# q and k of a dilated attention stored in three token orders, and score maxima over 65 rows instead of 64

## Chip, cores and metric

One core of one Trainium2 chip runs the whole program. The metric is the device time of one execution in microseconds (us), median over runs; lower is better.

## The reference

One encoder block on x of 1024 tokens and width 1024, all in float32. Cut to what the change touches, mixer A, an attention over strided neighbours:

```python
A_GROUPS = ((128, 1), (512, 4), (2048, 16))      # window, dilation; 4 heads of 64 per group

def dilated_group(q, k, v, window, dilation):
    L = S // dilation
    radius = window // (2 * dilation)            # 64 in all three groups
    def to_sub(t):
        return t.reshape(B, L, dilation, H, D).transpose(0, 2, 1, 3, 4).reshape(B * dilation, L, H, D)
    o, lse = banded_attention(to_sub(q), to_sub(k), to_sub(v), radius)
    ...

def mixer_dilated(qkv, pos):
    q, k = rotary(q, pos, ...), rotary(k, pos, ...)   # first 16 of 64 head dims
    ...                                               # 3 groups, combined by their softmax denominators
```

Around it: an input projection, a latent attention B with 8 heads, an output projection, and a feed-forward network with a squared relu.

## The kernel before

Products with large weights are split into a high and a low fp32r part, three matmuls for one, and run as a Strassen-like scheme of seven products (class `Seven`). The program has stages, one after the other: v and the rotary key (0 to about 97 us), the rest of the input projection, 17 units of 512 x 512 blocks (to 424.8 us), attention A with B's query projection woven in (to about 610 us), attention B, the output projection, and the feed-forward network.

**Projection units.** `proj.unit(u)` issues a unit's products in five steps and yields after each; the loop then issues a step of the next unit's operand preparation (`all_parts`: VectorE sums, a ScalarE cast to the high part, a GpSimd subtraction for the low part). Units 0 and 1 hold the rotary dims of q and k; in `put` a pair of their results takes 4 VectorE operations (L588 to L593) and 2 GpSimd products before it is stored. Units 2 to 5 hold the other q and k dims; `put` scales each of their four results with a VectorE product and stores it. Results lie as dims x tokens, in natural token order, in DRAM: `rx` (rotary) and `nx` (the rest).

**Attention A.** Four heads j, each with three groups g of dilation 1, 4 and 16 (g = 2 is computed as 8 residue classes with a parity mask). `load_qk(j, g)` brings Q and K (64 rows of dims, 1024 tokens) to SBUF; row 64 of K holds -1 and row 64 of Q the running maximum, so that the score product over 65 rows already subtracts it. For each head: `rounded` casts Q and K to fp32r; `maxima` multiplies the 64 rows and VectorE takes row maxima; `shift_a` turns them into Q's row 64, by 8 single-row operations for each group; `rows` copies that row to the Q of groups 1 and 2 by a DMA; `attend_a` computes scores (`scores`, two instructions for each fp32 product), exponentials, masks and the product with v. `shifts(j + 1)` is interleaved step by step with `attend_a(j)`, and between steps a fixed amount of TensorE work of B's query projection is issued (`ups.run`). The tokens of a block of g = 1 or 2 are 4 or 8 elements apart in Q and K:

```python
    def tokens(ap, g, b):
        ...
        d = 4 if g == 1 else 8
        v = ap.rearrange("p (i d) -> p d i", d=d)
        if g == 1:
            return v[:, b // 2, (b % 2) * P:(b % 2 + 1) * P]
        return v[:, b, :]
```

Each engine runs its instructions in the order of the program text; SyncE issues nearly all DMAs, in order.

Of the kernel before, what the change touches and what calls it, by code (L numbers as in the profile page):

```python
# [11 lines left out]
F32 = mybir.dt.float32  # L12
F32R = mybir.dt.float32r
# [4 lines left out]
P = 128  # L18
S = 1024
# [7 lines left out]
HA = 64  # L27
# [37 lines left out]
def tile_hybrid_block(ctx: ExitStack, tc: tile.TileContext, a: dict):  # L65
# [212 lines left out]


    vd = dram.tile([S, 6 * 192], F32, name="vd")  # L280
    rx = [dram.tile([192, S], F32, name=f"rx{i}") for i in range(2)]
    nx = dram.tile([1152, S], F32, name="nx")
    lat = [dram.tile([P, S], F32, name=f"lat{i}") for i in range(6)]


# [8 lines left out]
    X = {}  # L294
# [20 lines left out]
    halves = [slice(0, 512), slice(512, S)]  # L315
# [4 lines left out]
    def fetch_p(src):  # L320
        raw = raw_p(src.shape[-1])
        SP.dma_start(raw, src)
        return raw
# [180 lines left out]
    for k in range(HD):  # L504
# [1 line left out]
                      [lambda k=k: w_high("s3", W["a11"][k])],  # L506
                      [lambda k=k: w_low("s3", k, W["a11"][k])]])
    steps(items)
    proj = Seven(lambda u, e: fetch_p(a["w_p"][2 * u + e]), {n: (lambda k, n=n: (X[n][0][:, k], X[n][1][:, k]))
                  for n in ("b11", "b21", "b22", "t1", "t2", "t3", "t4")},  # L510
                 None, None, op_p, tmp_p, None)
    proj.fetch(0, 0, 1)
# [23 lines left out]

    NU = 17
    proj.first_parts(0)  # L540
    proj.first_parts(1)
    more = proj.all_parts(0, False)
# [30 lines left out]
    def scaled(u):  # L573

        return 2 <= u < 6 or u > 8

    def put(u, e, j, z, scale=True):

        tok = halves[j]
        if scale and scaled(u):  # L580
            V.tensor_mul(z, z, rbc[j])
        if u < 2:
            done[e, j] = z
            if (1 - e, j) in done:
                z1, z2 = done.pop((0, j)), done.pop((1, j))
                o = [tmp_p() for _ in range(4)]
                cos, sin = tabs[0][j], tabs[1][j]
                V.tensor_mul(o[0], z1, cos)  # L588
                G.tensor_mul(o[1], z2, sin)
                G.tensor_mul(o[2], z2, cos)  # L590
                V.tensor_mul(o[3], z1, sin)
                V.tensor_sub(o[0], o[0], o[1])
                V.tensor_add(o[2], o[2], o[3])  # L593
                for i, x in enumerate((o[0], o[2])):
                    SP.dma_start(rx[i][96 * u:96 * u + 96, tok], x[0:96])
                    n = 1024 + (2 * u + i) * 32
                    SP.dma_start(nx[n:n + 32, tok], x[96:128])
            return
        if u < 6:
            n = (2 * (u - 2) + e) * P  # L600
            SP.dma_start(nx[n:n + P, tok], z)
        elif u < 9:
            i = min(u - 6, 1)
            if u < 8 and e == j:
                C.activation(sums[i][j], z, AF.Square)
            else:
                s_ = work_p()
                C.activation(s_, z, AF.Square)
                G.tensor_add(sums[i][j], sums[i][j], s_)
            n = 2 * (u - 6) + e  # L610
            V.tensor_scalar(z, z, glat[:, n:n + 1], None, op0=ALU.mult)
            SP.dma_start(lat[n][:, tok], z)
        else:
            if last_unit:
                leave.append((zg[2 * (u - 9) + e][:, tok], z))
            else:
                SP.dma_start(zg[2 * (u - 9) + e][:, tok], z)

    def put_first(u, z):
        o = work_p()  # L620
        if scaled(u):
            V.tensor_mul(o, z, rbc[0])
        else:
            C.copy(o, z)
        put(u, 0, 0, o, False)

    proj.work, proj.first, proj.rest = work_p, put_first, put

# [13 lines left out]
    for u in range(NU):  # L642
        if u + 1 == NU:
            last_unit.append(u)
            for j in range(2):
                x = pop.tile([P, 512], F32, tag="op", name="rbc2", bufs=17)
                C.copy(x, rbc[j])
                rbc[j] = x
        if u + 2 < NU:
            proj.fetch(u + 2, 0, 1)  # L650
        more = proj.all_parts(u + 1, u + 1 >= 2) if u + 1 < NU else iter(())
        for _ in proj.unit(u, u >= 2, swap=u + 1 == NU):
            next(more, None)
            for _ in range(2):
                next(stats, None)
        if u == 0:
            put_first(1, proj.s1[1][0])
        if u == 9:
            stats = chain(mean_square(0, KVR, rkv), mean_square(1, QR, rq))
# [37 lines left out]
    def parts_g(raw, sub=G):  # L697
        return parts(raw, "wg", 1024, 4, sub)

    def tokens(ap, g, b):  # L700

        if g == 0:
            return ap[:, b * P:(b + 1) * P]
        d = 4 if g == 1 else 8
        v = ap.rearrange("p (i d) -> p d i", d=d)
        if g == 1:
            return v[:, b // 2, (b % 2) * P:(b % 2 + 1) * P]
        return v[:, b, :]


    QT, KTt, vt = {}, {}, {}

    def load_qk(j, g):
        for s_, (d, tag) in enumerate(((QT, "Q"), (KTt, "K"))):
            t_ = pqk.tile([HA + 1, S], F32, tag=tag, name=tag, bufs=5)
            d[j, g] = t_
            u = 6 * j + 3 * s_ + g
            for i in range(2):
                SP.dma_start(t_[8 * i:8 * i + 8], rx[i][8 * u:8 * u + 8])
            SP.dma_start(t_[16:HA], nx[48 * u:48 * u + 48])  # L720
        soon.append(lambda: G.memset(KTt[j, g][HA:HA + 1], -1.0))


    def load_v(g, pr):
# [10 lines left out]
        else:  # L735
            SP.dma_start(t_, src.rearrange("(p b) c -> p b c", b=TT))

    chores, soon = [], []
    q_raw, rots = {}, {}

    qd = [dram.tile([P, S], F32, name=f"qd{i}") for i in range(6)]
# [33 lines left out]
        return nq  # L775

    def rounded(j, g):
        qh = pr_.tile([HA, S], F32R, tag="qh", name="qh", bufs=2)
        kh = pr_.tile([HA, S], F32R, tag="kh", name="kh", bufs=2)
        (C.copy if (j, g) in ((0, 0), (0, 1), (2, 0)) else V.tensor_copy)(qh, QT[j, g][0:HA])  # L780
        C.copy(kh, KTt[j, g][0:HA])
        return qh, kh

    w_uq = [fetch(a["w_uq"][:, k * 768:k * 768 + 768]) for k in range(2)]
# [23 lines left out]
    for x in mgs:  # L808
        G.memset(x, 0.0)
    wuq += [parts(x) for x in w_uq[3:]]  # L810
    first = rounded(0, 0)
    while soon:
        soon.pop(0)()
    chores += [lambda: load_v(0, 0), lambda: load_qk(1, 0), lambda: load_qk(1, 1)]

    def band(b, n):
# [3 lines left out]
    def other(ap, g, b):  # L820

        n = TT if g == 0 else 2
        bb = b if g == 0 else b % 2
        lo, hi = band(bb, n)
        t0 = bb * P - 64 + lo
        if g == 0:
            return ap[:, t0:t0 + hi - lo]
        return ap.rearrange("p (i d) -> p d i", d=4)[:, b // 2, t0:t0 + hi - lo]


    def maxima(j, g, b0, qh, kh):

        n = 2 if g < 2 else 4
        pm = bank("ps_m").rearrange("p (b c) -> p b c", b=n)
        todo = []
        for b in range(b0, b0 + n):
            if g < 2:
                lo, hi = band(b if g == 0 else b % 2, TT if g == 0 else 2)
                mask, rhs = madd[:, lo:hi], other(kh, g, b)
            else:  # L840
                lo, hi, mask, rhs = 0, P, padd, tokens(kh, g, b)
            dst = pm[:, b % n, lo:hi]
            PE.matmul(dst, tokens(qh, g, b), rhs, start=True, stop=True)
            todo.append((b, dst, mask, hi - lo))
        for b, dst, mask, m in todo:
            junk = pa.tile([P, 256], F32, tag="junk", name="junk", bufs=1)
            V.tensor_tensor_reduce(out=junk[:, :m], in0=dst, in1=mask, scale=1.0, scalar=-BIG,
                                   op0=ALU.add, op1=ALU.max, accum_out=mgs[(3 * j + g) % 2][:, 32 * b:32 * b + 1])
# [16 lines left out]
                    V.tensor_max(mine, src, mine)  # L865

    def rows(j, g):
        SP.dma_start(QT[j, g][HA:HA + 1], QT[j, 0][HA:HA + 1])


    ROOM_MAX, ROOM_END, ROOM_SCORES = (800, 500, 460, 490), (2360, 2000, 2000, 1840), (260, 350, 350, 370)
# [19 lines left out]
    def attend_a(j):  # L891
# [21 lines left out]
        def scores(g, b0):  # L913
            pq = bank("ps_sA")
            pt = pa.tile([P, 512], F32, tag="pA", name="pA", bufs=4)
            q, k = QT[j, g], KTt[j, g]
            if g < 2:
                n = TT if g == 0 else 2
                for b in (b0, b0 + 1):
                    lo, hi = band(b if g == 0 else b % 2, n)  # L920
                    o = (b % 2) * 256
                    PE.matmul(pq[:, o + lo:o + hi], tokens(k, g, b), other(q, g, b), start=True, stop=True)
                f0 = band(b0 if g == 0 else 0, n)[0]
                f1 = 256 + band(b0 + 1 if g == 0 else 1, n)[1]
                C.activation(pt[:, f0:f1], pq[:, f0:f1], AF.Exp, scale=A_SCALE)
                keep_band(pt, f0, f1)
                return pt
            for b in range(b0, b0 + 4):
                o = (b % 4) * P
                PE.matmul(pq[:, o:o + P], tokens(k, g, b), tokens(q, g, b), start=True, stop=True)  # L930
            C.activation(pt, pq, AF.Exp, scale=A_SCALE)
            pt4 = pt.rearrange("p (b c) -> p b c", b=4)
            V.scalar_tensor_tensor(pt4, pt4, BIG, p01.unsqueeze(1).to_broadcast([P, 4, P]), op0=ALU.min, op1=ALU.mult)
            return pt
# [1216 lines left out]
```

## Time and profile before

| what | value |
|---|---|
| time, median of 3 runs (lowest to highest) | 1664.58 us (1663.78 to 1665.07) |
| the profiled execution: its time, its span | 1664.59 us, 1662.9 us |
| TensorE busy, share of the span | 1599.8 us, 96% |
| VectorE, ScalarE, GpSimd busy | 74%, 40%, 66% |
| moved by DMA | 208.16 MB, 125 GB/s |

The profile is of one execution. Engines are PE (TensorE matmuls), PEld (its weight loads, which overlap), DVE (VectorE), ACT (ScalarE), POOL (GpSimd) and SP (SyncE, which issues DMAs). L843 is line 843 of the kernel. Shares over the whole span hide the stages, so a change is read from the stage it lies in.

### The profile page before, as it was taken

The numbers are of one execution on the slowest core, as the hardware profiler recorded it, in microseconds if no ns is written. First come the engines' busy times: TensorE is split into PE (matmuls) and PEld (weight loads), VectorE is DVE, ScalarE is ACT, GpSimd is POOL, SyncE is SP. The second block draws the span as 40 slices with busy tenths as digits, with TensorE's granted clock in tenths as the row PEclk, the third lists the DMA queues.
The fourth block names the chain that finished last, engine by engine and source line by source line (L and its number), as shares of the span: only waits on it lengthen the run. The fifth ranks groups of instructions, "written<-read, shape, count | busy, mean of one in ns | idle before, by whom it ended". The sixth has DMA issues, their size and how long they took to land. (4 is left out here: it accounts for less than half of the span.)

```text
span 1662.9 us, 21207 instructions
## 1 busy us (share of the span) xinstructions
PE 1599.8 (96%) x7212; PEld 1327.3 (80%) x7212; DVE 1222.2 (74%) x1612; ACT 670.4 (40%) x1238; POOL 1103.7 (66%) x958
## 2 busy tenths in 40 slices
PE   7889999999999999999899999799999999999997
PEld 7778888888788887777678887688888888888886
DVE  8967556454646678889977267997776789889885
ACT  5732233222333347666666344322222363343421
POOL 7757457544724358777767346787777778888865
PEclk9899999999989899999999999899999999999999
DMA  6533233232644200000026243354434385445352
GB/s 231 165 124 129 108 108 116 94 126 101 192 128 121 67 17 20 20 1 20 20 99 224 101 165 114 122 178 176 146 140 158 139 310 164 140 141 160 119 201 101
DMA packets 85643, 208.16 MB, mean 125 GB/s; under 512 B 10472, under 2 KB 23968, under 8 KB 85536
## 3 DMA queue, kind: packets, MB, share of 16 engines
q1 hardware_dynamic: 85536, 206.82, 36.8%
q8 instruction: 57, 0.93, 0.2%
q14 instruction: 50, 0.41, 0.1%
HBM read 143.54 MB, written 63.18 MB: 124 GB/s over the span
## 5 line engine op out<-in xcount | busy, mean ns | idle before, releaser
L1276 POOL TENSOR_TENSOR pl<-pf,ph 128x512 fp32r<-128x512 f32 x124 | 168.4, 1364 | 56.7 <-DVE ph L1275 35.5
L103 POOL TENSOR_TENSOR op_p<-tS_p,op_p 128x512 fp32r<-128x512 f32 x68 | 94.9, 1416 | 103.6 <-ACT op_p L102 103.6
L1896 PE MATMUL ps_y<-opl,oph 128*128 128x512 f32 x364 | 141.8, 390 | 0.0
L1896 PE MATMUL ps_y<-oph 128*128 128x512 f32 x364 | 141.7, 389 | 0.0
L1896 PE MATMUL ps_y<-oph,opl 128*128 128x512 f32 x364 | 141.6, 389 | 0.0
L1981 DVE TENSOR_TENSOR R<-R,ps_y 128x1024 f32<-128x1024 f32 x84 | 100.8, 1213 | 22.6 <-PE ps_y L1896 22.4
L1854 DVE TENSOR_TENSOR opl<-raw_u,oph 128x512 fp32r<-128x512 f32 x91 | 110.5, 1242 | 7.3 <-ACT oph L1849 7.0
L103 POOL TENSOR_TENSOR opl<-tS,oph 128x512 fp32r<-128x512 f32 x61 | 94.1, 1562 | 28.3 <-ACT oph L102 24.5
L1271 ACT ACTIVATE pf<-ps_sB 128x512 f32<-128x512 f32 x128 | 76.6, 598 | 69.6 <-PE ps_sB L110 60.6
L102 ACT CAST op_p<-tS_p 128x512 fp32r<-128x512 f32 x68 | 39.9, 618 | 144.0 <-DVE tS_p L195 81.6
L1148 DVE TENSOR_REDUCE mx<-ps_mB 128x1 f32<-128x512 f32 x128 | 81.0, 682 | 17.0 <-PE ps_mB L1146 16.7
L103 POOL TENSOR_TENSOR op_p<-raw_p,op_p 128x512 fp32r<-128x512 f32 x51 | 72.8, 1433 | 21.2 <-ACT op_p L102 17.6
L1854 POOL TENSOR_TENSOR opl<-wk,oph 128x512 fp32r<-128x512 f32 x52 | 82.2, 1606 | 3.1 <-ACT oph L1849 2.9
L103 POOL TENSOR_TENSOR opl<-raw_f,oph 128x512 fp32r<-128x512 f32 x48 | 80.5, 1690 | 4.2 <-ACT oph L102 3.7
L1854 POOL TENSOR_TENSOR opl<-raw_f,oph 128x512 fp32r<-128x512 f32 x39 | 57.3, 1486 | 38.2 <-PE ps_y L1896 30.6
L1849 ACT CAST oph<-wk 128x512 fp32r<-128x512 f32 x52 | 32.3, 621 | 122.3 <-POOL wk L1821 49.3
L1896 PEld LDWEIGHTS ps_y<-opl,oph 128*128 128x128 f32 x364 | 68.3, 188 | 14.8 <-POOL opl L1854 0.6
L1896 PEld LDWEIGHTS ps_y<-oph 128*128 128x128 f32 x364 | 68.3, 188 | 14.6 <-ACT R L1985 0.5
L1896 PEld LDWEIGHTS ps_y<-oph,opl 128*128 128x128 f32 x364 | 68.3, 188 | 14.1
L152 PE MATMUL ps_zb<-Tl,oph 128*128 128x512 f32 x192 | 75.8, 395 | 2.7 <-DVE Tl L103 2.7
L151 PE MATMUL ps_zb<-Th,oph 128*128 128x512 f32 x192 | 75.7, 394 | 2.9 <-DVE wk L216 1.8
L153 PE MATMUL ps_zb<-Th,opl 128*128 128x512 f32 x192 | 75.7, 394 | 0.0
(492 smaller groups left out, 5174.5 us busy)
## 6 DMA issues: line engine op xcount, KB each, us to landing
raw_f<-in_w_ff SPq DMA_DIRECT2D x68, 512.0 KB
raw_u<-ua SPq DMA_DIRECT2D x39, 512.0 KB
raw_p<-in_w_p SPq DMA_DIRECT2D x34, 512.0 KB
ua<-su SPq DMA_DIRECT2D x26, 512.0 KB
ua<-uo SPq DMA_DIRECT2D x43, 256.0 KB
sg<-zg SPq DMA_DIRECT2D x32, 256.0 KB
zg<-wk SPq DMA_DIRECT2D x28, 256.0 KB
wk<-in_xT SPq DMA_DIRECT2D x16, 256.0 KB
```

Source lines behind the costliest of these rows:

```text
L102: C.copy(hi, src)
L103: (sub or V).tensor_sub(lo, src, f32(hi))
L151: PE.matmul(out, wh[:, c], bh, start=first and k == 0, stop=False, skip_group_check=True)
L152: PE.matmul(out, wh[:, c], bl, start=False, stop=False, skip_group_check=True)
L153: PE.matmul(out, wl[:, c], bh, start=False, stop=k == 3, skip_group_check=True)
L1148: V.reduce_max(mx[h][:, hf, t:t + 1], pq, axis=AX.X)
L1271: C.activation(pf, pq, AF.Exp, scale=B_SCALE)
L1276: sub.tensor_sub(pl, pf, f32(ph))
L1849: C.copy(hi, x)
L1854: eng.tensor_sub(lo, x, f32(hi))
L1896: PE.matmul(out, l[:, col], r_, start=first and p == 0 and e == 0, stop=p == len(CHUNKS[c]) - 1 and e == 2, skip_group_check=True)
L1981: V.tensor_add(acc, acc, py2)
```

## The change

1. `put_qk` stores every q and k result in three token orders. The natural order is stored at once. Two ScalarE copies, each to a fresh 128 x 512 buffer, put the tokens into the order of dilation 4 and 8 and store those; they are queued and issued when two steps of the unit loop have been counted (`turned_qk`), ahead of the next operand preparation. 48 copies and 64 stores are new.
2. The units run in the order 2, 3, 0, 4, 1, 5, then 6 to 16: the rotary units are third and fifth.
3. `load_qk` reads Q and K of a group in that group's order, for g = 2 by two DMAs in pieces of 64 tokens where one DMA read whole rows. `tokens` and `other` become contiguous slices.
4. `rows` is a ScalarE copy of one row into the group's order instead of a DMA.
5. `rounded` casts 65 rows, and so `maxima` multiplies 65. Q's row 64 is set to 0 by a GpSimd memset behind that of K's; the first `rounded` moves behind these memsets.

```diff
-    rx = [dram.tile([192, S], F32, name=f"rx{i}") for i in range(2)]
-    nx = dram.tile([1152, S], F32, name="nx")
+    rx = [[dram.tile([192, S], F32, name=f"rx{g}{i}") for i in range(2)] for g in range(3)]
+    nx = [dram.tile([1152, S], F32, name=f"nx{g}") for g in range(3)]
...
+    UNITS = [2, 3, 0, 4, 1, 5] + list(range(6, NU))
...
+    def put_qk(j, x, *to):
+        for dst, n, a, b in to:
+            SP.dma_start(dst[0][n:n + b - a, halves[j]], x[a:b])
+        def turn(g):
+            d = 4 * g
+            t_ = work_p()
+            C.copy(t_.rearrange("p (d i) -> p d i", d=d), x.rearrange("p (i d) -> p d i", d=d))
+            ...
+        turns.append([2, lambda: turn(1)])
+        turns.append([2, lambda: turn(2)])
...
         for _ in proj.unit(u, u >= 2, swap=u + 1 == NU):
+            turned_qk()
             next(more, None)
...
     def load_qk(j, g):
...
-                SP.dma_start(t_[8 * i:8 * i + 8], rx[i][8 * u:8 * u + 8])
-            SP.dma_start(t_[16:HA], nx[48 * u:48 * u + 48])
-        soon.append(lambda: G.memset(KTt[j, g][HA:HA + 1], -1.0))
+                fetch_rows(t_[8 * i:8 * i + 8], rx[g][i][8 * u:8 * u + 8], g)
+            fetch_rows(t_[16:HA], nx[g][48 * u:48 * u + 48], g)
+        def last_rows():
+            G.memset(KTt[j, g][HA:HA + 1], -1.0)
+            G.memset(QT[j, g][HA:HA + 1], 0.0)
+            has_rows.add((j, g))
+        soon.append(last_rows)
...
     def rounded(j, g):
-        qh = pr_.tile([HA, S], F32R, tag="qh", name="qh", bufs=2)
+        qh = pr_.tile([HA + 1, S], F32R, tag="qh", name="qh", bufs=2)
...
-    first = rounded(0, 0)
     while soon:
         soon.pop(0)()
+    first = rounded(0, 0)
...
-            PE.matmul(dst, tokens(qh, g, b), rhs, start=True, stop=True)
+            PE.matmul(dst, tokens(qh, b), rhs, start=True, stop=True)
...
     def rows(j, g):
-        SP.dma_start(QT[j, g][HA:HA + 1], QT[j, 0][HA:HA + 1])
+        d = 4 * g
+        src, dst = QT[j, 0][HA:HA + 1], QT[j, g][HA:HA + 1]
+        C.copy(dst.rearrange("p (d i) -> p d i", d=d), src.rearrange("p (i d) -> p d i", d=d))
```

**What moves on the engines.** First GpSimd at the start of attention A, around the memsets of K's row 64 (L721). Before:

```order
L103 TENSOR_TENSOR Wl<-raw,Wh 128x768
L721 MEMSET K 1x1024 x3
L103 TENSOR_TENSOR qp<-stage,qp 128x512 x2
L990 TENSOR_TENSOR ropes<-kpe,ropes 128x128
L991 TENSOR_TENSOR ropes<-kpe,ropes 128x4x16
```

With the change:

```order
L103 TENSOR_TENSOR Wl<-raw,Wh 128x768
L757 MEMSET K 1x1024
L758 MEMSET Q 1x1024
L757 MEMSET K 1x1024
L758 MEMSET Q 1x1024
L757 MEMSET K 1x1024
L758 MEMSET Q 1x1024
L103 TENSOR_TENSOR qp<-stage,qp 128x512 x2
```

Six memsets stand where three stood, and the cast that feeds the first maxima (qh, ScalarE) now waits for the first two of them, where it waited for no GpSimd instruction.

Second VectorE in the first unit, from the preparation of the next unit's sums (L195, L196) to the second unit's first result (the second L216). Before:

```order
L195 TENSOR_TENSOR tS_p<-raw_p 128x512
L196 TENSOR_TENSOR tS_p<-raw_p,tS_p 128x512
L232 TENSOR_TENSOR wk<-wk,ps_zc 128x512
L588 TENSOR_TENSOR tS_p<-wk 128x512
L591 TENSOR_TENSOR tS_p<-wk 128x512
L592 TENSOR_TENSOR tS_p<-tS_p 128x512
L593 TENSOR_TENSOR tS_p<-tS_p 128x512
L237 TENSOR_TENSOR wk<-wk,ps_zb 128x512
L588 TENSOR_TENSOR tS_p<-wk 128x512
L591 TENSOR_TENSOR tS_p<-wk 128x512
L592 TENSOR_TENSOR tS_p<-tS_p 128x512
L593 TENSOR_TENSOR tS_p<-tS_p 128x512
```

With the change:

```order
L195 TENSOR_TENSOR tS_p<-raw_p 128x512
L196 TENSOR_TENSOR tS_p<-raw_p,tS_p 128x512
L232 TENSOR_TENSOR wk<-wk,ps_zc 128x512
L614 TENSOR_TENSOR wk<-wk,oA 128x512
L237 TENSOR_TENSOR wk<-wk,ps_zb 128x512
L614 TENSOR_TENSOR wk<-wk,oA 128x512
L652 TENSOR_TENSOR wk<-ps_z_1007,oA 128x512
L216 TENSOR_TENSOR wk<-wk,ps_zb 128x512
```

Between L232 and the next L216 stand four operations, where nine stood.

## Rows read from the trace of the kernel before

**Rows 1.** The page, part 1: busy time of each engine, share, instructions.

```profile
PE 1599.8 (96%) x7212; PEld 1327.3 (80%) x7212; DVE 1222.2 (74%) x1612; ACT 670.4 (40%) x1238; POOL 1103.7 (66%) x958
```

**Rows 2.** Stretches: length; busy PE, PEld, DVE, ACT, POOL; clock, DMA share, GB/s.

```profile
117.00:124.00 7.00, 0.59 (x3) 0.18 (x2) 7.00 (x8) 0.00 (x0) 6.20 (x4) 0.69 0.28 83
124.00:130.00 6.00, 5.99 (x14) 4.73 (x15) 2.73 (x4) 1.66 (x3) 3.92 (x4) 0.51 0.72 218
130.00:160.00 30.00, 30.00 (x134) 24.83 (x133) 26.00 (x26) 7.38 (x13) 23.95 (x16) 1.00 0.37 121
...
425.00:451.00 26.00, 22.79 (x142) 19.61 (x141) 20.50 (x73) 8.96 (x18) 19.65 (x25) 1.00 0.76 206
...
454.00:468.00 14.00, 14.00 (x51) 11.42 (x50) 3.73 (x14) 2.67 (x4) 4.59 (x18) 0.51 0.77 237
...
498.50:539.80 41.30, 39.69 (x221) 34.31 (x222) 24.80 (x80) 13.62 (x25) 18.46 (x41) 1.00 0.43 122
...
570.00:581.00 11.00, 11.00 (x47) 10.55 (x47) 7.79 (x29) 1.71 (x4) 2.51 (x2) 0.53 0.00 1
```

**Rows 3.** TensorE's timeline, a step of group 0: start, length, engine, what.

```profile
500.33 1.03 PE L922 MATMUL ps_sA<-Q,K 65*128 65x256 f32 x4
501.29 0.50 PE L843 MATMUL ps_m<-kh,qh 64*128 64x256 f32 x2
501.72 0.38 PE L108 MATMUL ps_uq<-qp,Wh 128*128 128x256 f32 x1
501.94 0.28 PE L109 MATMUL ps_uq<-qp,Wh 128*128 128x256 f32 x1
502.06 0.28 PE L110 MATMUL ps_uq<-qp,Wl 128*128 128x256 f32 x1
```

**Rows 4.** TensorE's timeline, a step of group 1.

```profile
508.43 1.63 PE L922 MATMUL ps_sA<-Q,K 65*128 65x192 f32 x4
509.99 0.77 PE L843 MATMUL ps_m<-kh,qh 64*128 64x192 f32 x2
510.69 0.39 PE L108 MATMUL ps_uq<-qp,Wh 128*128 128x256 f32 x1
```

**Rows 5.** TensorE's timeline, a step of group 2.

```profile
523.71 2.12 PE L930 MATMUL ps_sA<-Q,K 65*128 65x128 f32 x8
525.76 1.21 PE L843 MATMUL ps_m<-kh,qh 64*128 64x128 f32 x4
526.90 0.39 PE L108 MATMUL ps_uq<-qp,Wh 128*128 128x256 f32 x1
```

**Rows 6.** TensorE's timeline, scores of the last head, before a 96-row product.

```profile
583.39 2.72 PE L922 MATMUL ps_sA<-Q,K 65*128 65x192 f32 x12
585.76 0.81 PE L1146 MATMUL ps_mB<-KTh,QTh 96*128 96x512 f32 x2
```

**Rows 7.** Timelines of ScalarE, VectorE and TensorE around TensorE's idle time in the projection.

```profile
102.94 1.07 ACT L569 COPY oA<-ps_r 128x512 f32<-128x512 f32 x2
...
113.58 1.78 DVE L592 TENSOR_TENSOR tS_p<-tS_p 128x512 f32<-128x512 f32 x1
...
117.20 0.39 PE L153 MATMUL ps_zc<-x_t1h,op_p 128*128 128x512 f32 x1
124.01 0.77 PE L151 MATMUL ps_zb<-x_t3h,op_p 128*128 128x512 f32 x1 [6.42 <-DVE wk L216]
```

**Rows 8.** ScalarE in the projection, 130 to 280 us, by line: busy us, mean ns.

```profile
L162 ACT COPY wk<-ps_z 128x512 f32<-128x512 f32 x8 | 4.7, 584 | 19.7 <-PE ps_z L153 19.7
```

**Rows 9.** The start of attention A, timelines of GpSimd, ScalarE and TensorE.

```profile
425.70 2.73 POOL L721 MEMSET K<- 1x1024 f32 x3
...
423.11 1.05 ACT L781 CAST kh<-K 64x1024 fp32r<-64x1024 f32 x1
...
424.76 0.49 PE L843 MATMUL ps_m<-kh,qh 64*128 64x192 f32 x2
```

**Rows 10.** A load for group 2 and the cast that needs it, timelines of SyncE and ScalarE.

```profile
507.18 0.62 SPq L719 DMA_DIRECT2D Q<-rx  x2
...
518.36 1.04 ACT L781 CAST kh<-K 64x1024 fp32r<-64x1024 f32 x1
```

More of the change, by code (lines that the diff above doesn't have):

```diff
@@ L508, in tile_hybrid_block @@
     steps(items)
-    proj = Seven(lambda u, e: fetch_p(a["w_p"][2 * u + e]), {n: (lambda k, n=n: (X[n][0][:, k], X[n][1][:, k]))
+    NU = 17
+    UNITS = [2, 3, 0, 4, 1, 5] + list(range(6, NU))
+    proj = Seven(lambda i, e: fetch_p(a["w_p"][2 * UNITS[i] + e]), {n: (lambda k, n=n: (X[n][0][:, k], X[n][1][:, k]))
                   for n in ("b11", "b21", "b22", "t1", "t2", "t3", "t4")},
@@ L535, in tile_hybrid_block @@
             SP.dma_start(x, a["rot_a"][i][:, h])
-    NU = 17
     proj.first_parts(0)
@@ L575, in scaled, with turned_qk, put @@
         return 2 <= u < 6 or u > 8
-    def put(u, e, j, z, scale=True):
+    turns = []
+    def put_qk(j, x, *to):
[5 more added lines that the diff above has]
+            C.copy(t_.rearrange("p (d i) -> p d i", d=d), x.rearrange("p (i d) -> p d i", d=d))
+            for dst, n, a, b in to:
+                rows = dst[g][n:n + b - a]
+                if g == 1:
+                    SP.dma_start(rows.rearrange("p (d j i) -> p d j i", d=d, j=2)[:, :, j],
+                                 t_[a:b].rearrange("p (d i) -> p d i", d=d))
+                else:
+                    SP.dma_start(rows[:, halves[j]], t_[a:b])
+        turns.append([2, lambda: turn(1)])
+        turns.append([2, lambda: turn(2)])
+    def turned_qk():
+        for t_ in turns:
+            t_[0] -= 1
+        while turns and turns[0][0] <= 0:
+            turns.pop(0)[1]()
+    def put(i, e, j, z, scale=True):
+        u = UNITS[i]
         tok = halves[j]
@@ L594, in put @@
                 for i, x in enumerate((o[0], o[2])):
-                    SP.dma_start(rx[i][96 * u:96 * u + 96, tok], x[0:96])
-                    n = 1024 + (2 * u + i) * 32
-                    SP.dma_start(nx[n:n + 32, tok], x[96:128])
+                    put_qk(j, x, ([r_[i] for r_ in rx], 96 * u, 0, 96), (nx, 1024 + (2 * u + i) * 32, 96, 128))
             return
         if u < 6:
-            n = (2 * (u - 2) + e) * P
-            SP.dma_start(nx[n:n + P, tok], z)
+            put_qk(j, z, (nx, (2 * (u - 2) + e) * P, 0, P))
         elif u < 9:
@@ L617, in put, with put_first @@
                 SP.dma_start(zg[2 * (u - 9) + e][:, tok], z)
-    def put_first(u, z):
+    def put_first(i, z):
         o = work_p()
-        if scaled(u):
+        if scaled(UNITS[i]):
             V.tensor_mul(o, z, rbc[0])
@@ L624, in put_first @@
             C.copy(o, z)
-        put(u, 0, 0, o, False)
+        put(i, 0, 0, o, False)
     proj.work, proj.first, proj.rest = work_p, put_first, put
@@ L698, in parts_g, with tokens, fetch_rows @@
         return parts(raw, "wg", 1024, 4, sub)
[L700 to L708, printed above, removed]
-    QT, KTt, vt = {}, {}, {}
+    def tokens(ap, b):
+        return ap[:, b * P:(b + 1) * P]
+    QT, KTt, vt = {}, {}, {}
+    def fetch_rows(dst, src, g):
+        if g == 2:
+            src = src.rearrange("p (j d i) -> p d j i", j=2, d=8)
+            dst = dst.rearrange("p (d j i) -> p d j i", j=2, d=8)
+            for h in range(2):
+                SP.dma_start(dst[:, :, h], src[:, :, h])
+            return
+        SP.dma_start(dst, src)
     def load_qk(j, g):
@@ L736, in load_v @@
             SP.dma_start(t_, src.rearrange("(p b) c -> p b c", b=TT))
-    chores, soon = [], []
+    chores, soon, has_rows = [], [], set()
     q_raw, rots = {}, {}
@@ L777, in rounded @@
     def rounded(j, g):
-        qh = pr_.tile([HA, S], F32R, tag="qh", name="qh", bufs=2)
-        kh = pr_.tile([HA, S], F32R, tag="kh", name="kh", bufs=2)
-        (C.copy if (j, g) in ((0, 0), (0, 1), (2, 0)) else V.tensor_copy)(qh, QT[j, g][0:HA])
-        C.copy(kh, KTt[j, g][0:HA])
+        assert (j, g) in has_rows
+        qh = pr_.tile([HA + 1, S], F32R, tag="qh", name="qh", bufs=2)
+        kh = pr_.tile([HA + 1, S], F32R, tag="kh", name="kh", bufs=2)
+        (C.copy if (j, g) in ((0, 0), (0, 1), (2, 0)) else V.tensor_copy)(qh, QT[j, g])
+        C.copy(kh, KTt[j, g])
         return qh, kh
@@ L827, in other @@
             return ap[:, t0:t0 + hi - lo]
-        return ap.rearrange("p (i d) -> p d i", d=4)[:, b // 2, t0:t0 + hi - lo]
+        return ap.rearrange("p (d i) -> p d i", d=4)[:, b // 2, t0:t0 + hi - lo]
     def maxima(j, g, b0, qh, kh):
@@ L840, in maxima @@
             else:
-                lo, hi, mask, rhs = 0, P, padd, tokens(kh, g, b)
+                lo, hi, mask, rhs = 0, P, padd, tokens(kh, b)
             dst = pm[:, b % n, lo:hi]
-            PE.matmul(dst, tokens(qh, g, b), rhs, start=True, stop=True)
+            PE.matmul(dst, tokens(qh, b), rhs, start=True, stop=True)
             todo.append((b, dst, mask, hi - lo))
@@ L921, in scores @@
                     o = (b % 2) * 256
-                    PE.matmul(pq[:, o + lo:o + hi], tokens(k, g, b), other(q, g, b), start=True, stop=True)
+                    PE.matmul(pq[:, o + lo:o + hi], tokens(k, b), other(q, g, b), start=True, stop=True)
                 f0 = band(b0 if g == 0 else 0, n)[0]
@@ L929, in scores @@
                 o = (b % 4) * P
-                PE.matmul(pq[:, o:o + P], tokens(k, g, b), tokens(q, g, b), start=True, stop=True)
+                PE.matmul(pq[:, o:o + P], tokens(k, b), tokens(q, b), start=True, stop=True)
             C.activation(pt, pq, AF.Exp, scale=A_SCALE)
```

## Prediction

> **What bounds the kernel now.** I read the page's engine line first: TensorE is busy 96% of the span, the next engine 74% [rows 1]. So a gain has to come out of TensorE's own time, or out of the few places where it waits. The table of stretches then shows the stages that the change touches: the projection, with one stretch where TensorE stands (117 to 124 us, 0.59 of 7 us busy), and attention A from 425 us on, with TensorE busy 39.69 of 41.30 us in the second head while VectorE has 24.80, ScalarE 13.62 and GpSimd 18.46 [rows 2]. A is bound by TensorE too, but by what? TensorE's timeline answers that. Starts of neighbouring rows tell what an instruction really costs, since the lengths overlap.
>
> Three things are to be seen there. **First**, a product over 64 rows does not overlap with its neighbours. Two products of 256 columns follow each other in 0.12 us (L109 to L110), but the pair of maxima takes 0.43 us (501.29 to 501.72), the first product behind it 0.22 instead of 0.12, and the four scores before it 0.96 us [rows 3]. Twelve contiguous scores in the last head (2 of 192 columns, 10 of 256, 2944 together) take 2.37 us, 0.805 ns for a column, and the 96-row product behind them starts without such a delay [rows 6]; by that price four of 256 columns take 0.82 us. So a group-0 call of maxima loses 0.19 + 0.10 + 0.14, about 0.4 us, to the change from and to 64 rows. The scores have 65 rows and lose nothing against 128-row neighbours. **Second**, strided reads cost more. Four group-1 scores of 192 columns take 1.56 us (508.43 to 509.99) where contiguous ones would take 4 x 0.155 = 0.62; a pair of maxima takes 0.70 [rows 4]. Eight group-2 scores take 2.05 us, 0.256 each; four maxima take 1.14 [rows 5]. **Third**, in the first projection unit VectorE works through a run of rotary operations at up to 1.78 us each, and the product that waits for it starts 6.42 us late [rows 7]; the 6 us behind it run at a granted clock of 0.51 [rows 2], the 1.2 GHz level.
>
> **The change, part by part.** The sum is made against the profiled execution, 1664.59 us, which is the median (1664.58) to 0.01 us.
>
> *Maxima and scores on TensorE.* Contiguous products of few columns cost no less than 0.12 us, the nearest row [rows 3]. There are 16 group-0 calls, 16 group-1 calls and 8 group-2 calls of maxima, and 16 and 8 groups of scores of groups 1 and 2.
> - Group-0 maxima: 16 x 0.4 = 6.4.
> - Group-1 maxima: 0.70 - 0.24 = 0.46, and 0.10 behind them: 16 x 0.56 = 9.0.
> - Group-2 maxima: 1.14 - 0.48 = 0.66, and 0.10: 8 x 0.76 = 6.1.
> - Group-1 scores: 1.56 - 0.62 = 0.94: 16 x 0.94 = 15.0.
> - Group-2 scores: 2.05 - 8 x 0.12 = 1.09: 8 x 1.09 = 8.7.
>
> That is 45.2 us at full clock. In the last head no maxima follow the scores (0.6 less), and stretches such as 454 to 468 and 570 to 581 us run at half clock [rows 2], where part of a slow read is hidden under slower columns. The ends are 39, if the groups in these 25 of A's 182 us gain nothing, and 45; I take 42, between them, since only a part is hidden. An extra 65th row costs nothing, as the 65-row scores show.
>
> *Units in another order.* The rotary operations leave the first unit, with five products of some 2.7 us; VectorE has four operations between L232 and L216 there instead of nine. The 6.42 us go, and 0.49 of the 6 us at half clock, 2.9 us: 9.3. What is late next: the first result is now scaled by VectorE with a factor that a ScalarE copy delivers only at about 103.5 us (102.94 plus half of 1.07) [rows 7], and L216 stands behind it. Nothing shows that wait before; it is between 0 and two contended VectorE operations, 3.6 us. I take 2. In the third and fifth unit the rotary run meets units of seven products, 19 us instead of 13.6. The second rotary unit of before, next to such a unit, left TensorE busy 30.00 of 30 us [rows 2], so I count 0 to 3 and take 1. Together -6.
>
> *48 ScalarE copies of 128 x 512, 8 in each of six units.* A contiguous copy takes 0.584 us [rows 8]. None with a step of 16 or 32 bytes is in the trace; below that price nothing is likely, and above it the nearest row is TensorE's own ratio for a step of 32 bytes, 0.256 to 0.12: 1.25 us. I take 0.8, nearer to the same engine's row: 6.4 us for each unit. The cover is ScalarE's idle time: it is busy 7.38 of 30 us [rows 2], 4.7 of a 19-us unit, and operands are prepared one unit ahead. So 0 on the path, at 1.25 us too (10 of 14.3 free). If the cover is gone, each copy is paid in full. The rows above show that strided reads are slow for TensorE. The Trainium skill, SBUF — State Buffer, section Door 1: The DMA port swizzle, gives 16-byte lines as the reason: reads that touch each line once pay a penalty, which would hold for these copies as well. It names no price for ScalarE, and with TensorE's ratio the sum would stay as it is; with a higher price it is the last rival below.
>
> *64 new stores and smaller loads.* The stores queue on SyncE, at about 0.31 us for an issue [rows 10]; no engine waits for them, except ScalarE for a buffer that comes round again. The load for a later head's group 2 has twelve DMAs instead of six. Two issues take 0.62 us, so the last one goes out some 2 us later; it starts at 507.18 and the cast that needs it ran at 518.36 [rows 10], 11 us later. Shorter steps leave about 8. Covered: 0; if not, 1 to 2 us for each of three heads.
>
> *Row copies and memsets.* Eight single-row ScalarE copies of 1024 elements, near the 1.05 us of a 64-row cast [rows 9], to 2.2 by the same ratio, lie under ScalarE's idle time in A (13.62 of 41.30 busy); so do 12 more memsets of 0.91 us on GpSimd (18.46 of 41.30) [rows 2]. 0.
>
> *The first maxima wait for memsets.* This is a new wait on the path. At 424.76 TensorE starts its first maxima, 0.6 us after the casts. The memsets start at 425.70 behind the last weight subtraction, at 0.91 us each [rows 9]. The casts now wait for two, until 427.5, and take 1.05 each, so TensorE starts at about 429.7: **5 us** late, and everything behind it in the queue with it. After 6.4 us of idle time the clock was at half for 6 us and 2.9 us were lost [rows 2]; I add 3. The ends are 4 and 12 (14 us at half clock, as at 454). Together +8.
>
> *Clock in A.* Stretches at 0.51 and 0.53 cost about half of 14 and 11 us, 12 us in all [rows 2]. The later one lies in strided group-2 steps, before which TensorE had not stood idle; with short steps it may go. Ends 0 and -12; I take -3.
>
> *New waits in A.* A head with 41.30 us loses 4 x (0.4 + 0.56 + 0.94) + 2 x (0.76 + 1.09) = 11.3, leaving 30 for 24.80 us of VectorE [rows 2], 83%. Some steps will wait for VectorE; ends 0 and 20, I take +5.
>
> Sum: -42 - 6 + 8 - 3 + 5 = **-38**, so 1664.6 - 38 = **1627 us**.
>
> **The rivals.**
> - *VectorE becomes the bound.* If it cannot go over 70% of a stretch, each of three heads stays at 24.8 / 0.7 = 35 us instead of 30, and 425 to 451 us, with VectorE already at 20.50 of 26, saves nothing of its 5.4: 20 us of waits instead of 5, **1642 us**. For it: those 20.50 us. Against: TensorE rarely waits for VectorE in A now, and at the end of a head only.
> - *The drain stays at 65 rows.* The maxima follow f32r products and the scores f32 ones, so the loss could hang on something else than 64 rows. Then 40 calls x 0.4 = 16 us stay: **1643 us**. The 65-row scores and the 96-row product [rows 6] speak against it. This is the case that the change does not do what it says.
> - *Everything is recovered.* The clock stays at full behind the first maxima and in A, and nothing new waits: -45 - 9 + 5 - 5 = -54, **1611 us**.
> - *The other side: ScalarE becomes the bound of the projection.* Its copies have room for 1.8 us each in four units and 1.28 in the first two (13.6 less 3.4 of other work, by 8). Beyond that TensorE pays 48 S - 78 for S us a copy; this eats the 38 us from S = 2.4, four times a contiguous copy. At 3 us it is +66, **1693 us**. For it speaks that strided reads are slow and that no row prices them on ScalarE; against, that TensorE's own ratio is 2.1, half of what it takes.
>
> **How the numbers follow.** The chances are 0.50 for the forecast (its own range 1619 to 1635), 0.20 for VectorE, 0.08 for the drain, 0.15 for full recovery, 0.05 for ScalarE, and 0.02 for a mixture that ends near no change. The range of 0.8 reaches from 1612, just short of full recovery, to 1646, over the two cases near 1642. About 0.2% (3.3 us) is what a measurement of this kernel can tell from no change. All cases but the last two lie below 1661: faster 0.93, same 0.02, slower 0.05.
>
> **What would show it.** In the profile of the changed kernel: group-1 and group-2 scores four and eight in about 0.65 and 0.95 us; maxima in 0.12 us each, with no delay behind them; no idle 6.4 us near 117; a ScalarE copy under 1.3 us; TensorE idle for about 5 us before its first maxima; VectorE at 80% or more of each head. The prediction is wrong if maxima over 65 rows still take 0.2 us each, if the copies take over 2 us, or if A shortens by less than 20 us.

## Result, and the profile after

The changed kernel takes **1640.38 us** (median of 4 runs, 1633.53 to 1643.42) against 1664.78 us for the kernel before, run beside it: ratio 0.985, 95% interval 0.9817 to 0.988. The forecast was 1627 us, so 24 of the 38 us arrived. The profiled execution took 1641.31 us with a span of 1639.4 us, 23.4 us less than before.

The page, part 1, of the changed kernel, answers to [rows 1]:

```profile
PE 1566.1 (96%) x7212; PEld 1306.0 (80%) x7212; DVE 1231.2 (75%) x1612; ACT 738.6 (45%) x1294; POOL 1120.5 (68%) x970
```

TensorE's busy time fell by 33.7 us and the span by 23.4: some 10 us more of it are idle. To see where, I cut both traces at the first maxima and at the first scores of B. The table of stretches (columns as in [rows 2]) for attention A before:

```profile
424.76:613.74 188.98, 181.93 (x948) 158.38 (x947) 116.41 (x348) 62.52 (x129) 84.08 (x205) 0.92 0.37 106
```

And after, with the projection's stretches, then A, then four stretches within A:

```profile
117.00:124.00 7.00, 7.00 (x33) 5.79 (x32) 5.56 (x6) 7.00 (x9) 4.80 (x4) 1.00 0.98 292
124.00:130.00 6.00, 6.00 (x28) 4.99 (x27) 4.49 (x5) 4.54 (x8) 5.97 (x5) 1.00 0.91 317
...
421.02:590.43 169.41, 154.25 (x946) 146.03 (x947) 116.48 (x346) 79.37 (x137) 92.34 (x212) 0.83 0.41 115
446.40:460.10 13.70, 13.70 (x55) 12.78 (x53) 4.92 (x19) 6.93 (x7) 5.77 (x18) 0.50 0.79 245
483.90:497.60 13.70, 13.70 (x55) 12.94 (x55) 6.00 (x20) 7.12 (x7) 5.33 (x18) 0.50 0.45 140
521.40:535.10 13.70, 13.70 (x55) 12.62 (x53) 8.87 (x23) 8.32 (x8) 7.52 (x19) 0.50 0.58 159
559.00:572.70 13.70, 13.70 (x45) 12.25 (x46) 6.61 (x10) 7.76 (x9) 7.45 (x23) 0.50 0.18 49
```

A shrank by 19.6 us only. Three numbers in its two rows say why. TensorE's idle time (length less busy) rose from 7.05 to 15.16 us, +8.1. The clock's loss (length times what the granted clock lacks to 1.00) rose from 0.08 x 188.98 = 15.1 to 0.17 x 169.41 = 28.8, +13.7. What is left is 19.6 + 8.1 + 13.7 = 41.4 us of TensorE work saved, where the forecast had 42. So the saving is all there, and 22 us were given back. The four last rows hold most of the clock's part: in each TensorE is busy without a gap for 13.70 us, at the 1.2 GHz level. They begin within 2 us of a head's first scores, which start at 444.84, 482.07, 519.65 and 558.98.

The working takes every instruction in such a stretch to be slower by the clock. Strided reads were not: before, eight group-2 scores took 2.01 us in a stretch at half clock (571.61 to 573.62), and 2.05 at full clock [rows 5]:

```profile
571.61 2.08 PE L930 MATMUL ps_sA<-Q,K 65*128 65x128 f32 x8
573.62 1.22 PE L843 MATMUL ps_m<-kh,qh 64*128 64x128 f32 x4
```

By an estimate from the strided steps in the stretches at half clock of before, some 3 us pass from one term to the other: 44 us of work saved, 16 given back by the clock.

The kernel before had a stretch of 13.7 us behind head 0's scores too [rows 2]. Besides, it had three with no idle time over 0.2 us in the 20 us ahead of them:

```profile
484.86:488.27 3.41, 3.41 (x16) 3.41 (x15) 1.70 (x9) 1.41 (x3) 2.30 (x2) 0.50 0.27 99
563.36:566.78 3.42, 3.42 (x9) 2.87 (x10) 0.77 (x5) 0.58 (x1) 0.90 (x5) 0.50 0.02 5
570.19:580.43 10.24, 10.24 (x42) 9.89 (x42) 7.17 (x28) 1.62 (x3) 2.51 (x2) 0.50 0.00 0
```

In the changed kernel these three are gone. So +13.7 is a sum: three gone (-8.5), three new ones behind the scores of heads 1 to 3 (+20.5), and one of 3.4 us behind the first maxima (+1.7).

The steps themselves, on TensorE's timeline: one of group 1 and one of group 2, answering to [rows 4, 5].

```profile
504.03 0.81 PE L964 MATMUL ps_sA<-Q,K 65*128 65x192 f32 x4
504.55 0.50 PE L883 MATMUL ps_m<-kh,qh 65*128 65x192 f32 x2
504.88 0.60 PE L1120 MATMUL ps_r<-ident,rkv 128*128 128x128 f32 x4
...
506.32 1.06 PE L972 MATMUL ps_sA<-Q,K 65*128 65x128 f32 x8
507.13 0.64 PE L883 MATMUL ps_m<-kh,qh 65*128 65x128 f32 x4
507.61 0.34 PE L108 MATMUL ps_uq<-qp,Wh 128*128 128x256 f32 x1
```

By starts, four group-1 scores take 0.52 us (1.56 before), eight group-2 scores 0.81 (2.05), four maxima 0.48 (1.14).

Next the head change. VectorE's timeline, then TensorE's:

```profile
475.53 3.24 DVE L902 TENSOR_TENSOR Q<-ps_mT,Q 1x128 f32<-1x128 f32 x8
478.80 3.17 DVE L905 TENSOR_TENSOR Q<-ps_mT,Q 1x128 f32<-1x128 f32 x8
482.00 1.29 DVE L1063 TENSOR_TENSOR qs<-ps_uq,rot_b 128x512 f32<-128x512 f32 x2
```
```profile
478.31 1.06 PE L944 MATMUL ps_oA<-pA,v 128*128 128x128 f32 x8
482.07 0.40 PE L964 MATMUL ps_sA<-Q,K 65*128 65x192 f32 x1 [2.71 <-issue]
```

Sixteen single-row folds (L902 for group 1, L905 for group 2; each takes one block's maxima into Q's row 64) run one after the other on VectorE for 6.4 us, and the scores start when the last is done. TensorE has run out of work 2.71 us before that. Its idle time ahead of the first scores of heads 0 to 3 was 2.15, 1.52, 1.59 and 0.03 us before and is 2.19, 2.71, 2.70 and 3.12 us now: it reaches the head change earlier, and VectorE does not. Heads 0 to 2 before, then heads 0, 2 and 3 now:

```profile
451.15 1.02 PE L922 MATMUL ps_sA<-Q,K 65*128 65x192 f32 x4 [2.15 <-DVE Q L865]
498.52 0.99 PE L922 MATMUL ps_sA<-Q,K 65*128 65x192 f32 x4 [1.52 <-issue]
539.80 0.99 PE L922 MATMUL ps_sA<-Q,K 65*128 65x192 f32 x4 [1.59 <-issue]
```
```profile
444.84 1.02 PE L964 MATMUL ps_sA<-Q,K 65*128 65x192 f32 x4 [2.19 <-DVE Q L905]
519.65 0.99 PE L964 MATMUL ps_sA<-Q,K 65*128 65x192 f32 x4 [2.70 <-issue]
558.98 1.82 PE L964 MATMUL ps_sA<-Q,K 65*128 65x192 f32 x4 [3.12 <-issue]
```

Of the 8.1 us more idle time in A, 5.4 lie at the head changes.

Last the start of A, timelines of GpSimd and TensorE, answering to [rows 9]:

```profile
417.11 0.95 POOL L757 MEMSET K<- 1x1024 f32 x1
...
417.28 0.39 PE L153 MATMUL ps_zc<-x_b22h,op_p 128*128 128x512 f32 x1
421.02 0.49 PE L883 MATMUL ps_m<-kh,qh 65*128 65x192 f32 x2 [3.35 <-ACT kh L821]
```

### The profile page after: what moved, and what is told of

It reads as the page before. It is cut to its first block, busy times and chain, and to the rows that moved or that the text cites. A ratio compares the mean times of both kernels' runs of the same rounds, so it can differ in the third digit from the quotient of the medians.

```text
span 1639.4 us, 21480 instructions
## 1 busy us (share of the span) xinstructions
PE 1566.1 (96%) x7212; PEld 1306.0 (80%) x7212; DVE 1231.2 (75%) x1612; ACT 738.6 (45%) x1294; POOL 1120.5 (68%) x970
## 5 line engine op out<-in xcount | busy, mean ns | idle before, releaser
L1190 DVE TENSOR_REDUCE mx<-ps_mB 128x1 f32<-128x512 f32 x128 | 81.0, 682 | 21.0 <-PE ps_mB L1188 20.5
```

The costliest lines, as they stand in the source:

```text
L1190: V.reduce_max(mx[h][:, hf, t:t + 1], pq, axis=AX.X)
```

## The experiments

My theory: the head change costs twice, by the idle time and by the clock behind it. Rivals: VectorE's work bounds A as a whole; the drain is not fully gone; the copies sit on the path. Each run below changes the changed kernel, or the kernel before where it says so.

**The late fold, a step earlier.**

```diff
-                if g and n == 1:
+                if g == 1 and n == 1 or g == 2 and n == 0:
                     shift_a(j, g - 1)
```

> Group 1's row of maxima is folded in after the first step of group 2 instead of the second, so that only group 2's eight folds are left after a head's last maxima. Theory (the head change holds the clock): TensorE's idle before the first scores of heads 0 to 3, 2.2 to 3.1 us each in the changed kernel, falls under 1 us, the four stretches of 13.7 us at 1.2 GHz that follow them vanish, and the time falls by 20 to 32 us, to 1608 to 1620 us. Rival (VectorE's work bounds the whole of A, the idle is only where that shows): the wait moves to another place, first maxima to the sparse stage's end stays at 169 us within 3, the time 1637 to 1643 us.

Measured: 1627.17 us (1625.61 to 1628.85), ratio to before 0.9771 (0.9756 to 0.9787). A's row in the table of stretches, and TensorE's timeline at two waits:

```profile
420.61:574.71 154.10, 136.46 (x947) 129.19 (x947) 116.15 (x346) 79.09 (x137) 91.41 (x212) 0.94 0.45 123
```
```profile
466.54 0.69 PE L883 MATMUL ps_m<-kh,qh 65*128 65x128 f32 x2 [4.16 <-ACT kh L821]
...
479.70 1.02 PE L964 MATMUL ps_sA<-Q,K 65*128 65x192 f32 x4 [0.23 <-DVE Q L905]
```

Ahead of the first scores TensorE now idles 1.19 us in head 0 and 0.23 in head 1, and not at all in heads 2 and 3. The four stretches are gone (four of 3.4 to 6.8 us are left, elsewhere), and A is 15.3 us shorter: the clock's loss falls from 28.8 to 0.06 x 154.10 = 9.2. The gain is 13 us and not 20 to 32, because other waits move up: a cast now waits for the load of the next head's group 2, 4.16 us, and idle time in A is 17.6 us, more than in the changed kernel. VectorE is busy 75% of A here and 69% in the changed kernel, and 30.70 of 34.00 us here in head 2:

```profile
512.00:546.00 34.00, 30.44 (x201) 27.77 (x200) 30.70 (x87) 19.96 (x32) 20.12 (x43) 0.95 0.44 111
```

So its throughput did not bound A in the changed kernel.

**The same wait, with TensorE kept busy.**

```diff
         yield ROOM_END[j]
+        idle = bank("ps_m")
+        for b in range(12):
+            PE.matmul(idle[:, b % 4 * P:b % 4 * P + P], tokens(KTt[j, 2], b % TT), tokens(KTt[j, 2], b % TT), start=True, stop=True)
```

> Twelve extra products of K with itself, 128 columns each and read by nobody, are put on TensorE ahead of each head's first scores, about as long as the idle there (2.2 to 3.1 us). The wait for VectorE's row stays. Theory (the idle costs twice, by itself and by the clock after it): the stretches of 13.7 us at 1.2 GHz vanish, at half of each some 6.9 us are given back, four times: 1613 to 1627 us. Rival (the clock falls for the work of the stretch, not for the idle before it, or VectorE bounds the stretch so that the clock costs nothing): 1638 to 1646 us with the same stretches, or without them and with the time unchanged.

Measured: 1628.52 us (1625.75 to 1630.68). TensorE's timeline at a head change, and A's row:

```profile
481.80 2.84 PE L934 MATMUL ps_m<-K 65*128 65x128 f32 x24
484.48 0.92 PE L967 MATMUL ps_sA<-Q,K 65*128 65x192 f32 x4
```
```profile
422.50:577.68 155.18, 141.67 (x1043) 136.22 (x1044) 115.55 (x346) 78.94 (x137) 91.56 (x212) 0.97 0.44 122
```

This tells the two halves of the cost apart. The useless products take 2.7 to 2.9 us of each head change (481.80 to 484.48 here), about as long as the idle time in whose place they stand, and the scores still start after them; yet 12 us are won, though the time lies 1.5 us above the theory's range. All of it is the clock: its loss falls by 24 us, to 0.03 x 155.18 = 4.7. A is 14.2 us shorter and not 24, because idle time turns up in other places; the longest is again the cast for head 1's group 2:

```profile
469.52 1.11 PE L883 MATMUL ps_m<-kh,qh 65*128 65x128 f32 x4 [4.70 <-ACT kh L821]
```

Both edits point to the idle time as what the four half-clock stretches of the changed kernel follow from.

**64 rows again, and 65 rows alone.** In the changed kernel the products read `qh[0:HA]` and `kh[0:HA]`; in the kernel before, the casts and the memsets are those of the change and nothing else is.

```diff
-            PE.matmul(dst, tokens(qh, b), rhs, start=True, stop=True)
+            PE.matmul(dst, tokens(qh[0:HA], b), rhs, start=True, stop=True)
```

> The changed kernel with the maxima's products over 64 rows again, all else (token orders, copies, units) kept. Theory: the drain between 64 and 65 rows comes back, 0.3 to 0.4 us at each of 40 groups of maxima, 12 to 16 us of TensorE time; against it, with slower maxima TensorE reaches the head change later, so that its idle there falls from 2.7 us towards 1.6 us and some of the half-clock stretches go: net 1630 to 1652 us, with maxima pairs 0.3 us longer and shorter idle before the scores. Rival (the drain has nothing to do with the rows, or is hidden behind VectorE): idle before the scores and half-clock time as in the changed kernel, the time 1637 to 1643 us.

> The kernel before the change with one part of it alone: the maxima's products over 65 rows (the last rows set to 0 and -1 ahead of the first casts), the token orders, copies, units and row loads as before. Theory (65 rows take the drain away, some 10 us of the sparse stage net in the changed kernel, by the run that put 64 rows back; the memsets ahead of the first casts stall the start by 3.35 us; the faster maxima lengthen the idle before each head's scores): the sparse stage shorter by 5 to 12 us, its start 3 to 5 us later, the time 1655 to 1663 us. Rival (the drain in the kernel before comes from the strided token orders, not from the rows): maxima pairs as long as before, 1666 to 1670 us for the start's stall alone.

Measured: 1650.45 us (1644.88 to 1658.86) with 64 rows back, and 1655.69 us (1652.93 to 1661.17) for 65 rows alone, ratio to before 0.9952 (0.9936 to 0.9968). A's row for the first, then for the second:

```profile
421.70:600.96 179.26, 168.12 (x947) 145.84 (x947) 115.85 (x346) 79.55 (x137) 90.76 (x212) 0.83 0.39 107
```
```profile
426.69:606.33 179.64, 171.16 (x946) 163.05 (x947) 115.84 (x346) 62.39 (x129) 92.08 (x212) 0.89 0.37 105
```

By the same working (length, idle time, clock), going back to 64 rows adds 9.9 us to A while idle time falls by 4.0 and the clock's loss rises by 1.7: 12.2 us of work. On the kernel before, 65 rows take 9.3 us from A, with 1.4 more idle time and 4.7 more lost to the clock: 15.4 us. The forecast was 16. The hope that slower maxima would end the half-clock stretches was wrong: 2.1 to 2.6 us of idle time are left ahead of each head, and each has a half-clock stretch of 13.7 or 17.1 us beside it. The Trainium skill, TensorEngine Tiling (Array Packing), section Tiling Modes, says that a change of row tiling drains the array, 64 rows being a tiling of its own; both runs agree.

**The units in their own order, and the copies contiguous** (which leaves the reordering of tokens out).

```diff
-    UNITS = [2, 3, 0, 4, 1, 5] + list(range(6, NU))
+    UNITS = [0, 1, 2, 3, 4, 5] + list(range(6, NU))
```

> The changed kernel with the projection's units in their own order again (the two rotary units first). Theory (the order took away 9.3 us of waiting and cost some 3 us elsewhere): TensorE's wait of about 6.4 us ahead of 124 us comes back, the projection ends 5 to 8 us later, 1645 to 1649 us. Rival (the gap was closed by something else in the change, or a later wait takes it all): 1638 to 1642 us.

```diff
-            C.copy(t_.rearrange("p (d i) -> p d i", d=d), x.rearrange("p (i d) -> p d i", d=d))
+            C.copy(t_, x)
```

> The 48 ScalarE copies of q and k read and write in one order, contiguous, so the reordering of tokens for groups 1 and 2 is left out; stores, loads and all else are kept. Theory (the copies are hidden behind the projection's products): ScalarE's copies fall from 1.16 to about 0.58 us, the projection's end moves by under 2 us, the time stays at 1637 to 1643 us. Rival (copies delay the casts that TensorE waits for): the projection ends 5 to 20 us sooner, 1620 to 1635 us.

Measured: 1649.84 us (1645.82 to 1649.99) and 1640.26 us (1638.89 to 1641.34). TensorE's timeline with the units in their own order shows the wait of [rows 7] again:

```profile
124.14 0.77 PE L151 MATMUL ps_zb<-x_t3h,op_p 128*128 128x512 f32 x1 [6.45 <-DVE wk L216]
```

ScalarE's groups by line (line, operation, shapes, count, busy us and mean ns) in the projection of the changed kernel, then with contiguous copies, for 32 of the 48 copies:

```profile
L591 ACT COPY wk<-wk 128x512 f32<-128x512 f32 x32 | 35.6, 1157 | 9.4 <-DMA nx<-wk 6.2 <-DVE wk L614 3.0 <-DVE wk L652 0.3
```
```profile
L591 ACT COPY wk<-wk 128x512 f32<-128x512 f32 x32 | 19.1, 620 | 19.3 <-DMA nx<-wk 12.4 <-DVE wk L614 6.5 <-DVE wk L652 0.3
```

The order of the units is worth 9.5 us in the medians. Of this 7.0 lie between the first product of the units and the first maxima (324.2 us against 331.1); 1.5 lie ahead of the units, where the code is the same in both. The copies are hidden: 25 us less of ScalarE's work move the time by 0.1 us.

**The first memsets ahead of the weights**, alone and with the early fold.

```diff
+    soon.pop(0)()
     mgs = [pa.tile([P, 256], F32, name=f"mg{i}") for i in range(2)]
```

> The two memsets of the first Q's and K's last rows are issued on POOL ahead of the weights' splits, where POOL waits for nothing but a load. Theory (the stall of 3.35 us at the sparse stage's start is ScalarE's cast waiting for them): first maxima 3 to 3.5 us sooner after the projection's end, and up to 1.7 us more from the 3.4 us at half clock behind it: 1635 to 1638 us. Rival (the weights' splits, now 1.9 us later, hold the first products or the background work instead): 1639 to 1642 us.

> Group 1's fold a step earlier and the first memsets ahead of the weights' splits, together. Theory (the two waits are apart in time and add): 13 us from the head changes as measured, and 3 to 5 us from the start: 1622 to 1625 us. Rival (the loads of head 1's group 2, which held TensorE for 4.2 us in the version with the early fold, bound the first two heads, so that an earlier start only lengthens that wait): 1626 to 1629 us.

Measured: 1639.47 us (1637.72 to 1641.54) alone and 1625.01 us (1622.33 to 1627.95) with the fold. TensorE's timeline, memsets alone, at the start of A, at head 0's scores and at the longest wait of A:

```profile
417.49 0.39 PE L153 MATMUL ps_zc<-x_b22h,op_p 128*128 128x512 f32 x1
417.71 0.39 PE L884 MATMUL ps_m<-kh,qh 65*128 65x192 f32 x2
...
440.93 1.02 PE L965 MATMUL ps_sA<-Q,K 65*128 65x192 f32 x4 [2.17 <-DVE Q L906]
...
463.56 0.69 PE L884 MATMUL ps_m<-kh,qh 65*128 65x128 f32 x2 [4.36 <-ACT kh L821]
```

The stall is gone to the last tenth, and the time hardly moves: in the profiled execution the first maxima are 3.3 us sooner, at 417.71, and the span's end 1.8. The runs don't show even that: the ratio to before is 0.9856 (0.9839 to 0.9873), that of the changed kernel 0.985 (0.9817 to 0.988). The rival had the time but not the reason. What was won went into a cast of head 1, which waits for the load of its group 2: idle time in A is 4.5 us longer, against 3.4 less lost to the clock. Part of this clock is a surprise. Head 0's scores come after 2.17 us of idle time, as in the changed kernel, but no stretch at half clock follows:

```profile
441.00:460.90 19.90, 18.19 (x134) 17.57 (x134) 9.25 (x35) 10.97 (x18) 11.39 (x33) 1.00 0.80 232
```

With the early fold the median is 2.2 us under that of the fold alone, but the two sets of runs overlap, and beside the kernel before the ratios are 0.9769 and 0.9771: no gain over the fold alone is shown.

**The load that is late next.**

```diff
-            if i == 5 and j + 1 < NJ:
+            if i == 4 and j + 1 < NJ:
                 load_qk(j + 1, 2)
```

> The version with the early fold and the first memsets ahead of the weights, and with the loads of the next head's group 2 issued one of its steps sooner (the fifth step of the head before, not the sixth). Theory (a cast that waits for these loads holds TensorE for 4.0 us in head 1 and is what is late next): 2 to 4 us of that idle and up to 3.4 us of the half-clock stretch behind it go, 1619 to 1623 us. Rival (the transfers, not their issue, are late, or VectorE's folds hold head 1 anyway): 1624 to 1628 us.

Measured: 1623.80 us (1621.30 to 1627.49), ratio to before 0.9759 (0.9745 to 0.9773). The wait of 4.0 us in head 1 is gone, but a stretch of 13.7 us at half clock is back in head 0, at 442.4 us, where the version without the earlier load had 3.4 us, from 437.1. So it doesn't settle whether the load is worth moving. The three versions with the early fold are all faster than both kernels, at 1624 to 1627 us; among themselves the runs don't tell them apart.

**The early fold in the kernel before.**

> The kernel before the change with the fold of group 1 a step earlier, nothing else. Theory (the late fold holds the head change wherever TensorE arrives first; before the change it idled 2.2, 1.5, 1.6 and 0.0 us there, and only the 2.2 us were followed by 13.7 us at half clock): 4 us of idle and up to 7 us of clock, 1655 to 1662 us, so less than the 13 us that the same edit gave the changed kernel. Rival (the fold is worth the same in both, so it says nothing of why the change fell short): 1650 to 1653 us.

Measured: 1659.50 us (1656.99 to 1667.45), ratio 0.9978 (0.9965 to 0.9991): 4 us, against 13 in the changed kernel. The fold mattered little as long as TensorE came late to the head change. In the profiled execution (1663.20 us, above the median) idle time ahead of the four first scores falls from 5.3 to 1.9 us, and the clock's loss in A doesn't fall: 0.09 x 188.00 = 16.9 us, against 15.1.

```profile
424.31:612.31 188.00, 183.18 (x948) 159.36 (x947) 117.35 (x349) 62.61 (x129) 83.62 (x204) 0.91 0.37 106
```

So in the kernel before, half clock is not tied to that idle time as it is in the changed one.

## Why the prediction was right in its work and short in its sum

- **Maxima and scores, -42: right.** 41.4 us by A's rows. 65 rows take the drain away (12 to 15 us in two runs, 16 forecast). The rest is put down to the contiguous order: the steps' rows give 16 x 1.04 + 8 x 1.24 = 26.6 us for the scores; no run changed the order alone. The rival of the drain falls.
- **Units in another order, -6: about right**, 7.0 us in the profiled stage. The waits foreseen behind it are 1.00 us at 103.55 (forecast 2) and 0.35 and 0.31 later (forecast 1).
- **48 copies, 0: right on the path, the price off.** 1.157 us, not 0.8; the upper end, from TensorE's ratio, was 1.25. The same copies contiguous take 0.620, a ratio of 1.87. The trace agrees, for ScalarE's reads too, with the rule of 16-byte lines that the prediction takes from the Trainium skill, SBUF — State Buffer, section Door 1: The DMA port swizzle. The rival that needed 2.4 us falls.
- **The first maxima's wait, +8: too much.** 3.35 us idle, forecast 5, and 3.4 us at half clock behind it, 1.7 for the forecast 3. GpSimd comes to its memsets at 417.11, before the last product of the projection ends at 417.67; the forecast had them 0.94 us behind the first maxima's time, as in [rows 9]. With the memsets moved the first maxima come 3.3 us sooner, but later waits take nearly half of that in the profiled execution, and the runs show no gain.
- **Stores, loads, row copies and memsets, 0: held.** The load of a later head's group 2 holds TensorE only in versions that reach it sooner, 4.0 to 4.7 us in head 1.
- **Clock in A, -3 (ends 0 and -12): the step that failed, with the wrong sign.** Together with the 3 behind the start the forecast was 0; measured +13.7. What the term named came true: the later stretch, at 570 us, is gone, with two short ones (-8.5). What failed is that it asked only which stretches would go, and put none behind the new waits in A. I counted the clock behind the wait for the first maxima, but did not look at what stood ahead of the stretch from 454 us [rows 2]: TensorE's idle 2.15 us before the first scores of head 0. Three more such stretches cost 20.5 us. I had seen that TensorE waits for VectorE "at the end of a head only", and took it as a point against the rival; it was the place where the change would put its waits.
- **New waits in A, +5 (ends 0 and 20): mis-sized**, +8.1, of which 5.4 at the head changes and not spread over the steps.

The pieces: -41.4 + 13.7 + 8.1 + 3.35 - 7.0 = -23.2, with +1.3 in the rest of the projection and -1.4 ahead of the units, where nothing was changed; -23.4 was measured. The time lies at the rival "VectorE becomes the bound" (1642 us), but not by its mechanism: VectorE is at 69% of A in the changed kernel and went to 75% when the fold was moved. A serial run of sixteen small operations at one place of the dependence chain held TensorE, with VectorE far from full. So it is luck that the stated range holds the time: it reached to 1646 us for the two rivals near 1642, and neither happened; the forecast's own range ended at 1635.

Two of the prediction's own signs came out against it. A shortens by 19.6 us, and under 20 was to mean wrong: the work went as foreseen, but what was given back ate half of it. And VectorE was to be at 80% or more of each head; it is at 66% of head 1 (482 to 520 us).

## What to carry to other kernels

When TensorE's steps get shorter, look at the places where it already waits a little for a serial chain on another engine: those waits can grow by up to what the steps lose, and the clock can make each of them dearer than its own length (here 2.7 us idle, and 6.8 by the clock). Carry both costs in the sum until a trace shows full clock behind the stall. And remove one stall with a look at what is late next: of 3.35 us taken away at the start of A, 1.8 reached the end of the profiled execution, and the runs show no gain at all.

## What I had not expected of the hardware

- After 2.2 to 3.1 us without work ahead of a head's scores, the granted clock is 0.50 for 13.7 us, while TensorE is busy for all of these 13.70 us. In the kernel before, 1.5 and 1.6 us in the same place had no such stretch behind them.
- The length of one idle time alone does not decide it. With the first memsets moved, 2.17 us ahead of head 0's scores had full clock behind them up to 460.9 us. With the early fold TensorE stood still for 2.69 us ahead of 508.45 (it waited for the row maxima, before a transpose), and no such stretch followed. The longer wait for the first maxima, 3.35 us, had 3.4 us at half clock behind it, not 13.7. In the version with the earlier load, 1.25 us ahead of head 0's scores, 4.4 us after a wait of 2.15 us, came just before a stretch of 13.7 us; and three shorter stretches of the kernel before had no idle time over 0.2 us in the 20 us ahead of them. What decides was not tried further and stays open.
- Half the clock cost these strided products nothing: eight group-2 scores, their tokens read with a step of 32 bytes, took 2.01 us at half clock and 2.05 at full.
